# Chunked SSD outputs: log of dt in the exponent, the mask on GpSimd, u times v stored as one product, and earlier chunk loads

## The chip, the cores and the metric

The kernel runs on one core of one Trainium2 chip. The core has five instruction queues that run beside each other, each in its own fixed order: TensorE (PE, with its weight loads as PEld), VectorE (DVE), ScalarE (ACT), GpSimd (POOL) and SyncE (SP), which here only issues transfers. The metric is the device time of one execution in microseconds (us). The order on each queue is settled when the program is built, by a list scheduler that works with priorities, so a change in one place can reorder others.

## The reference

One layer of a two-stream trunk over 256 context tokens and 1024 latent tokens, D = 1024, float32: modulated RMSNorm, one input projection whose columns feed three mixers (Mamba-2 SSD, chunked spatial gating, S5), an output projection, a squared-ReLU MLP, a final norm. The change concerns two of the mixers. The SSD mixer, per direction and chunk of 128 tokens:

```
dt   = softplus(s[..., OFF_DT:OFF_SGU] + ssd_dt_bias)
a_cum = cumsum(dt * a)                                  # within a chunk
lmat = exp(where(lower, a_cum[q] - a_cum[k], -inf))
y_diag = sum_k (cm[q] . bm[k]) * lmat[q, k] * (x[k] * dt[k])
y_off  = (cm[q] . h_prev) * exp(a_cum[q])
h      = exp(a_cum[-1]) * h_prev + sum_k bm[k] * exp(a_cum[-1] - a_cum[k]) * x[k] * dt[k]
```

Both directions are summed (the backward one is masked the other way), and D times x is added. The gating mixer returns `u * mix`, with `mix = W_s v + b` per chunk and head.

## The kernel before, in words

Tokens lie along the free axis in ten chunks of 128; features lie on the partitions. A *slab* is 128 output columns of a projection for all 1280 tokens: 24 matmuls of 256 columns and 48 of 512 (`proj_tile`, three products of split operands for each of eight k).

Around the change the program runs: the v and dt projection (`vdt`), the spatial mix (`sgu_mix`), two slabs for u (`u_slab`), the S5 scans (`s5_main`, eight rounds), four xBC slabs (`xbc_slab`) and `dt_chain`, which makes dt and its running sums. Then `ssd_group` for two groups of four heads. Each group has a pass `right` that builds the backward states and a pass `outputs` over ten chunks. Group 0 is drawn first, four more xBC slabs stand between its two passes, and z slabs, the S5 gate, two mixed tiles (`mixed_tile`) and the first output-projection slabs are emitted among the output chunks. The code's order sets priorities; the scheduler interleaves.

One output chunk does this. It loads `xc` (x, B, C of the chunk) and `rb`, the running sums of both directions as rows, copied to all partitions: 512 KB from the DRAM tile `rows_d`. ACT makes `er = exp(rb)`. The decay matrix is the exponent min(row 0 - col 0, row 1 - col 1): per head one ACT shift of row 1 and one DVE subtract-and-min, then one ACT exponential over 128x512. The matmul B.C lands in PSUM (`pcb`); DVE multiplies it with the two triangular masks (`cm`), and per head ACT scales the one with dt of the forward direction and DVE adds the other scaled with dt of the backward one. DVE multiplies decay and this, and `rb[:, 1]` feeds four matmuls into `py` (tile ps_wb). `po` is the states' part; DVE multiplies it with `er`, POOL adds its two directions, DVE adds all into `cm`, which is stored to `y_d`. The forward state `hf` goes on to the next chunk: POOL scales it, DVE adds the new part.

Buffers: `rb` has 3, `xc` 5, `cm` 2. `rb` is held until the matmuls into `py` have read it. All these loads and the store go through SP's one queue in order. The mix goes to the DRAM tile `mix_d` in ten stores, gelu(u) to `u_d` from ACT's queue, and `mixed_tile` loads both and multiplies them.

In the profile every `tensor_tensor` has line 54, every `scalar_tensor_tensor` line 57, every activation line 60 and every DMA line 48, since helpers record them; they are told apart by their tiles.

Of the kernel before, what the change touches and what calls it, by code (L numbers as in the profile page):

```python
# [18 lines left out]
KD = 8  # L19
# [23 lines left out]
def trunk_kernel(ctx: ExitStack, tc: tile.TileContext, I, O):  # L43
# [3 lines left out]
    def load(dst, src, eng=None):  # L47
        (eng or nc.sync).dma_start(out=dst, in_=src)
# [190 lines left out]
    def ev(name, dt=F32):  # L239
        return evp.tile([128, 512], dt, tag="ev", name=name, bufs=7)  # L240
# [467 lines left out]

    def sgu_mix():
        for v in va:  # L710
            act(v, v, ACT.Gelu_apprx_tanh)
        for c in range(NCH):
            vq = ev("vq")[:, 0:256]
            act(vq, va[c // 5][:, c % 5, :], ACT.Square, accum_out=vss[:, c:c + 1])
        rstd(vss, vr, 256)
        for c in range(NCH):
            v = va[c // 5][:, c % 5, :]
            V.tensor_scalar(out=v, in0=v, scalar1=vr[:, c:c + 1], scalar2=None, op0=ALU.mult)
            pm = bank("mm", 2)
# [3 lines left out]
            mx = ev("vq")[:, 0:256].rearrange("p (a b) -> p a b", a=2)  # L723
            for a in range(2):
                stt(mx[:, a, :], pm[:, a * 128:(a + 1) * 128], sgug[:, a:a + 1], sgub[:, a, :], ALU.mult, ALU.add)
            load(mix_d.rearrange("(a p) n -> p a n", p=128)[:, :, c * 128:(c + 1) * 128], mx)

# [6 lines left out]
    def dt_chain():  # L734
# [32 lines left out]
        T.matmul(pc[:, 320:480], lhsT=ones, rhs=dta.rearrange("p d c -> p (d c)"), start=True, stop=True)  # L767
        S.copy(col[:, 0], pc[:, 0:80])
        act(col[:, 1], pc[:, 80:160], ACT.Copy, scale=-1.0)
        act(wdec.rearrange("p d c -> p (d c)"), pc[:, 160:320], ACT.Exp)  # L770
# [10 lines left out]

    def u_slab(m):
# [45 lines left out]

    def ssd_group(pool, g):

        hb = {1: None}

        def chunk_xbc(c, n):
            o = xoff(c)
            xc = pool.tile([128, 4, 128], F32, tag="xc", name="xc", bufs=5)[:, 0:n]
            load(xc, xbc_d[g, 0:n, :, o:o + 128].rearrange("a p n -> p a n"))
            return xc

        def scal(t, d, c):
            return t[:, d, c * 8 + g * 4:c * 8 + g * 4 + 4]  # L840
# [28 lines left out]
        def right():  # L869
            px, bt, _ = tok_major(chunk_xbc(1, 3))  # L870
            hb[0] = new_state(f"hb{g}", 9, 1, 1, px, bt, None, "hb")
# [4 lines left out]
            hb[9] = init(1, f"hb{g}", 9)  # L876
            yield
            for c in range(9, 2, -1):
                px, bt, _ = tok_major(chunk_xbc(c, 3))
                hb[c - 1] = new_state(f"hb{g}", 9, 1, c, px, bt, hb[c], "hb")  # L880
                yield

        def outputs():
            hf = None
            for c in range(NCH):
# [19 lines left out]
                cm = pool.tile([128, 2, 128], F32, tag="cm", name="cm", bufs=2)  # L905
                tt(cm, pcb.unsqueeze(1).to_broadcast([128, 2, 128]), tri[:, 0:2], ALU.mult)

                d0, d1 = scal(DTD, 0, c), scal(DTD, 1, c)
                for hh in range(4):
                    act(rb[:, 0, hh], cm[:, 0], ACT.Copy, scale=d0[:, hh:hh + 1])  # L910
                    stt(rb[:, 0, hh], cm[:, 1], d1[:, hh:hh + 1], rb[:, 0, hh], ALU.mult, ALU.add)
                tt(rb[:, 1], rb[:, 1], rb[:, 0], ALU.mult)
                xs = pool.tile([128, 4, 64], F32, tag="xs", name="xs", bufs=2)
                S.copy(xs, px)
                py = bank("wb", 2)[:, 0:256].rearrange("p (a q) -> p a q", a=2)
                for a in range(2):
                    for par in range(2):
                        T.matmul(py[par * 64:(par + 1) * 64, a, :], lhsT=xs[:, 2 * a + par], rhs=rb[:, 1, 2 * a + par],
                                 start=True, stop=True)
# [22 lines left out]
    def mixed_tile(t):  # L942
# [62 lines left out]
    with tc.tile_pool(name="pv", bufs=1) as pv, tc.tile_pool(name="p5", bufs=1) as p5, ExitStack() as stk:  # L1005
# [44 lines left out]
        V.tensor_scalar(out=glubh, in0=glub, scalar1=0.5, scalar2=None, op0=ALU.mult)  # L1050
        sgu_mix()
        for m in range(2):
            u_slab(m)
        for _ in prep:
# [21 lines left out]
    with tc.tile_pool(name="pd", bufs=1) as pd, banks("psB"):  # L1076
        (right0, out0), (right1, out1) = [ssd_group(pd, g) for g in range(2)]
        def drain(g):
# [536 lines left out]
```

## Time and profile before

| | us |
|---|---|
| median of 3 runs (lowest to highest) | 1580.24 (1580.15 to 1582.12) |
| the profiled execution | 1578.67 |
| its span on the core | 1576.7 |

| stretch (us from the span's start) | what runs | PE busy | granted clock, of full |
|---|---|---|---|
| 190 to 320 | S5 scans, xBC slabs | 121.82 of 130 | 0.97 |
| 320 to 390 | backward states of group 0, xBC and z slabs | 67.16 of 70 | 1.00 |
| 390 to 593 | the twenty output chunks, with z slabs and mixed tiles | 156.25 of 203 | 0.83 |
| 593 to 690 | output projection, second norm | 94.47 of 97 | 1.00 |

From 800 us on the MLP runs, with PE busy nearly throughout. The granted clock is a mean over the stretch; its levels are 1.2 and 2.4 GHz.

### The profile page before, as it was taken

Reading aid. Unit: us, or ns where it says so; the run is one execution under the profiler, and the core shown is the slowest. Engines: PE = TensorE matmul, PEld = TensorE weight load, DVE = VectorE, ACT = ScalarE, POOL = GpSimd, SP = SyncE. Lnnn points to the kernel's source line nnn. Section 1 sums busy time; section 2 is a strip of 40 time slices with the busy share of each in tenths; the row PEclk is TensorE's granted clock in tenths of the full one; section 3 lists DMA queues with packets and bytes.
Section 4 is the critical chain, followed back from the end, with each engine's and each line's share of the span. In section 5 each row is a group of like instructions: output and inputs, shape, how many; then the busy total and the mean of one; then the engine's idle time right before and its main releaser. Section 6 shows DMA issues by size and latency. Waiting matters only on the chain.

```text
span 1576.7 us, 23817 instructions
## 1 busy us (share of the span) xinstructions
PE 1423.4 (90%) x8360; PEld 1202.6 (76%) x8360; DVE 1067.9 (68%) x1929; ACT 751.1 (48%) x1541; POOL 389.5 (25%) x487
## 2 busy tenths in 40 slices
PE   4689898999787779989999999999899999999795
PEld 3567676778565568878888888888788888887795
DVE  5773368668667885558977764674564768979945
ACT  3643434456645753437655554554555334424322
POOL 4555466613011122321100000000241313032033
PEclk9699999999997879999999999999999999999897
DMA  9759785264675647346444443344744245315312
GB/s 326 251 174 252 227 285 159 88 171 119 181 228 149 172 145 236 122 123 195 138 158 149 149 139 116 125 148 151 250 149 146 70 158 174 121 54 182 112 35 100
DMA packets 238903, 253.29 MB, mean 161 GB/s; under 512 B 15648, under 2 KB 163136, under 8 KB 238784
## 3 DMA queue, kind: packets, MB, share of 16 engines
q1 hardware_dynamic: 222880, 234.51, 48.2%
q10 hardware_dynamic: 15904, 17.27, 3.4%
q8 instruction: 66, 1.08, 0.3%
q14 instruction: 53, 0.43, 0.1%
HBM read 182.82 MB, written 68.89 MB: 160 GB/s over the span
## 4 chain that ended last, share of the span: by engine, by line
PE 58%; DVE 8%; DMA 6%; ACT 2%; issue 2%; POOL 1%; SPq 0%; DVEq 0%; ACTq 0%; POOLq 0%
PE ps_w L1215 7%; PE ps_w L1213 7%; PE ps_w L1214 7%; PE ps_w L1369 6%; PE ps_w L1370 6%; PE ps_w L1371 6%; PE ps_mm L219 4%; PE ps_mm L221 4%; PE ps_mm L220 4%; DMA rb<-rows_d 2%; PE ps_mm L1371 1%; PE ps_mm L1370 1%; PE ps_mm L1369 1%; DVE X L54 1%; DVE rb L57 1%
## 5 line engine op out<-in xcount | busy, mean ns | idle before, releaser
L219 PE MATMUL ps_mm<-hi,wh 128*128 128x512 f32 (+1 forms) x576 | 211.6, 367 | 20.1 <-DVE dtr L707 16.0
L221 PE MATMUL ps_mm<-hi,wl 128*128 128x512 f32 (+1 forms) x576 | 209.4, 364 | 0.9 <-DVE wl L54 0.9
L220 PE MATMUL ps_mm<-lo,wh 128*128 128x512 f32 (+1 forms) x576 | 209.8, 364 | 0.0
L1369 PE MATMUL ps_w<-uB,uA 128*128 128x512 f32 (+1 forms) x520 | 190.6, 371 | 9.3 <-ACT uB L60 8.9
L1370 PE MATMUL ps_w<-uB,uA 128*128 128x512 f32 (+1 forms) x520 | 191.3, 368 | 7.9 <-DVE uB L54 7.9
L1371 PE MATMUL ps_w<-uB,uA 128*128 128x512 f32 (+1 forms) x520 | 190.2, 367 | 0.0
L54 POOL TENSOR_TENSOR cb<-h 128x512 f32<-128x512 f32 x14 | 21.9, 1571 | 512.7 <-DMA h<-w 402.4
L219 PEld LDWEIGHTS ps_mm<-hi,wh 128*128 128x128 f32 x576 | 111.2, 193 | 38.1 <-DVE dtr L707 16.8
L221 PEld LDWEIGHTS ps_mm<-hi,wl 128*128 128x128 f32 x576 | 111.0, 193 | 18.1 <-DVE wl L54 1.8
L220 PEld LDWEIGHTS ps_mm<-lo,wh 128*128 128x128 f32 x576 | 111.0, 193 | 15.0 <-issue 0.6
L1369 PEld LDWEIGHTS ps_w<-uB,uA 128*128 128x128 f32 x520 | 99.9, 193 | 25.2 <-ACT uB L60 9.3
L1370 PEld LDWEIGHTS ps_w<-uB,uA 128*128 128x128 f32 x520 | 100.2, 193 | 24.7 <-DVE uB L54 9.8
L1371 PEld LDWEIGHTS ps_w<-uB,uA 128*128 128x128 f32 x520 | 99.8, 192 | 15.5
L60 ACT ACTIVATE uB<-tb 128x512 fp32r<-128x512 f32 x106 | 65.9, 625 | 64.9 <-PE ps_w L1371 31.7
L54 DVE TENSOR_TENSOR uB<-tb,uB 128x512 fp32r<-128x512 f32 x106 | 87.6, 846 | 13.1 <-ACT uB L60 13.1
L54 DVE TENSOR_TENSOR X<-X,ps_w 128x512 f32<-128x512 f32 x84 | 56.1, 680 | 27.7 <-PE ps_w L1371 27.6
L54 DVE TENSOR_TENSOR q<-q,ps_w 128x512 f32<-128x512 f32 x48 | 32.9, 685 | 59.7 <-PE ps_w L1215 59.0
L54 DVE TENSOR_TENSOR wl<-wraw,wh 128x1024 fp32r<-128x1024 f32 x32 | 48.4, 1514 | 36.7 <-ACT wh L60 35.9
L60 ACT ACTIVATE c<-c 128x512 f32<-128x512 f32 x64 | 40.3, 629 | 57.8 <-DVE c L54 56.9
L1371 PE MATMUL ps_mm<-ch,uA 128*128 128x256 f32 x224 | 63.2, 283 | 0.0
L1370 PE MATMUL ps_mm<-cl,uA 128*128 128x256 f32 x224 | 63.2, 283 | 0.0
L1369 PE MATMUL ps_mm<-ch,uA 128*128 128x256 f32 x224 | 63.1, 283 | 0.0
(435 smaller groups left out, 3875.3 us busy)
## 6 DMA issues: line engine op xcount, KB each, us to landing
rw<-w SPq DMA_DIRECT2D x112, 256.0 KB
tb<-a_d SPq DMA_DIRECT2D x106, 256.0 KB
aw<-ada_w SPq DMA_DIRECT2D x64, 256.0 KB
h<-w SPq DMA_DIRECT2D x32, 512.0 KB
a_d<-t SPq DMA_DIRECT2D x42, 256.0 KB
rb<-rows_d SPq DMA_DIRECT2D x20, 512.0 KB
adaw<-ada_w SPq DMA_DIRECT2D x32, 256.0 KB
wraw<-w_out SPq DMA_DIRECT2D x16, 512.0 KB
```

Of the source, the lines that this page charges most:

```text
L54: eng.tensor_tensor(out=out, in0=a, in1=b, op=op)
L57: V.scalar_tensor_tensor(out=out, in0=a, scalar=sc, in1=b, op0=op0, op1=op1)
L60: S.activation(out=out, in_=in_, func=func, **kw)
L219: T.matmul(out, lhsT=wh(k), rhs=xh(k), start=(k == 0), stop=False)
L220: T.matmul(out, lhsT=wh(k), rhs=xl(k), start=False, stop=False)
L221: T.matmul(out, lhsT=wl(k), rhs=xh(k), start=False, stop=(k == nk - 1))
L1213: T.matmul(out, lhsT=wh, rhs=X[0][:, j, :], start=(j == 0), stop=False)
L1214: T.matmul(out, lhsT=wh, rhs=X[1][:, j, :], start=False, stop=False)
L1215: T.matmul(out, lhsT=wl, rhs=X[0][:, j, :], start=False, stop=(j == 3))
L1369: T.matmul(out, lhsT=wh, rhs=bh, start=start, stop=False)
L1370: T.matmul(out, lhsT=wh, rhs=bl, start=False, stop=False)
L1371: T.matmul(out, lhsT=wl, rhs=bh, start=False, stop=stop)
```

## The change

The exponent now carries log dt: `col` holds log(max(dt, 1e-37)) minus the running sum, for both directions. The mask is an additive tile `cap`, 0 where a pair counts and -1e30 where it doesn't, added to the rows by POOL, a direction at a time. ACT takes the exponential per head and direction with `col` as its bias; DVE adds the two directions and multiplies by B.C from PSUM. The result lies in `sg` (2 buffers), not in `rb`; `rb` has 2 buffers instead of 3, and is read only by POOL and by the exponentials for `er`. `cm` has 3 buffers instead of 2, and both groups' backward states share one ring of 16. The chunk loads of `xc` and `rb` get a priority 600 higher. The mix stays in SBUF, in two buffers of the pool that held x; `u_slab` multiplies it in and stores the product once, through SP's queue; `mixed_tile` loads one tile where it loaded two and multiplied.

```diff
-    def sgu_mix():
+    def sgu_mix(px):
+        mix = [px.tile([128, KD, 256], F32, tag="x", name="mix", bufs=2).rearrange("p k n -> p (k n)")[:, 0:NT]
+               for _ in range(2)]
...
-            load(mix_d.rearrange("(a p) n -> p a n", p=128)[:, :, c * 128:(c + 1) * 128], mx)
...
+        V.tensor_scalar(out=col, in0=DTD, scalar1=1e-37, scalar2=None, op0=ALU.max)
+        act(col, col, ACT.Ln)
+        fl = col.rearrange("p d c -> p (d c)")
+        tt(fl, fl, pc[:, 0:160], ALU.subtract)
...
             act(us, p, ACT.Gelu_apprx_tanh)
-            load(u_d[m * 128:(m + 1) * 128, t0:t0 + n], us, nc.scalar)
+            tt(us, us, mix[m][:, t0:t0 + n], ALU.mult)
+            load(um_d[m * 128:(m + 1) * 128, t0:t0 + n], us)
...
-                rb = pool.tile([128, 2, 4, 128], F32, tag="rb", name="rb", bufs=3)
-                load(rb, rows_d[:, c * 8 + g * 4:c * 8 + g * 4 + 4, :].partition_broadcast(128))
-                cf, cbk = scal(col, 0, c), scal(col, 1, c)
+                rb = pool.tile([128, 2, 4, 128], F32, tag="rb", name="rb", bufs=2)
+                with tc.high_priority(offset=600):
+                    load(rb, rows_d[:, c * 8 + g * 4:c * 8 + g * 4 + 4, :].partition_broadcast(128))
+                sg = pool.tile([128, 2, 4, 128], F32, tag="sg", name="sg", bufs=2)
+                for d in range(2):
+                    tt(sg[:, d], rb[:, d], cap[:, d].unsqueeze(1).to_broadcast([128, 4, 128]), ALU.add, G)
...
-                for hh in range(4):
-                    act(rb[:, 1, hh], rb[:, 1, hh], ACT.Identity, bias=cbk[:, hh:hh + 1])
-                    stt(rb[:, 1, hh], rb[:, 0, hh], cf[:, hh:hh + 1], rb[:, 1, hh], ALU.subtract, ALU.min)
-                act(rb[:, 1], rb[:, 1], ACT.Exp)
+                for d in range(2):
+                    cd = scal(col, d, c)
+                    for hh in range(4):
+                        act(sg[:, d, hh], sg[:, d, hh], ACT.Exp, bias=cd[:, hh:hh + 1])
+                tt(sg[:, 0], sg[:, 0], sg[:, 1], ALU.add)
...
-                tt(cm, pcb.unsqueeze(1).to_broadcast([128, 2, 128]), tri[:, 0:2], ALU.mult)
-                for hh in range(4):
-                    act(rb[:, 0, hh], cm[:, 0], ACT.Copy, scale=d0[:, hh:hh + 1])
-                    stt(rb[:, 0, hh], cm[:, 1], d1[:, hh:hh + 1], rb[:, 0, hh], ALU.mult, ALU.add)
-                tt(rb[:, 1], rb[:, 1], rb[:, 0], ALU.mult)
+                tt(sg[:, 0], pcb.unsqueeze(1).to_broadcast([128, 4, 128]), sg[:, 0], ALU.mult)
...
-            load(mx, mix_d[k * 128:(k + 1) * 128, t0:t0 + n])
-            tt(u, u, mx, ALU.mult)
...
+        cap = pd.tile([128, 2, 128], F32, name="cap")
+        V.tensor_scalar(out=cap, in0=tri[:, 0:2], scalar1=-1.0, scalar2=1e30, op0=ALU.add, op1=ALU.mult)
```

The order on every queue is the same up to the spatial mix and again from the second norm on. Between them it differs. On POOL, in the output pass of group 1 (er: the states' part; hf: the forward state; sq: the mixed tile's norm), before:

```order
L54 TENSOR_TENSOR hf<-hf,dtot 128x256
L54 TENSOR_TENSOR sq<-sq,z 128x256
L54 TENSOR_TENSOR er<-er 128x256
L54 TENSOR_TENSOR sq<-sq,z 128x256
L54 TENSOR_TENSOR hf<-hf,dtot 128x256
L54 TENSOR_TENSOR er<-er 128x256
L54 TENSOR_TENSOR hf<-hf,dtot 128x256
```

And now, around the same mixed tile:

```order
L54 TENSOR_TENSOR sg<-rb,cap 128x512 x2
L54 TENSOR_TENSOR sq<-sq,z 128x256
L54 TENSOR_TENSOR er<-er 128x256
L54 TENSOR_TENSOR hf<-hf,dtot 128x256
L54 TENSOR_TENSOR sq<-sq,z 128x256
L54 TENSOR_TENSOR sg<-rb,cap 128x512 x2
L54 TENSOR_TENSOR er<-er 128x256
L54 TENSOR_TENSOR hf<-hf,dtot 128x256
L54 TENSOR_TENSOR sg<-rb,cap 128x512 x2
```

Two adds of 128x512 stand in front of each chunk's `er` and `hf`; eight of the forty stand ahead of the first `hf`.

On PE, at the last output chunk (ps_wb: its matmuls; ps_mm with hi and wh: slab matmuls, three to each k), before:

```order
L219 MATMUL ps_mm<-hi_5688,wh 128x512
L220 MATMUL ps_mm<-lo_5689,wh 128x512
L221 MATMUL ps_mm<-hi_5688,wl 128x512
L918 MATMUL ps_wb<-rb,xs 64x128 x4
L925 MATMUL ps_wb<-xc,hf 128x128 x2
L925 MATMUL ps_wb<-xc,h_4442 128x128 x2
L219 MATMUL ps_mm<-hi_5688,wh 128x512
```

And now:

```order
L922 MATMUL ps_wb<-sg,xs 64x128 x4
L929 MATMUL ps_wb<-xc,hf 128x128 x2
L929 MATMUL ps_wb<-xc,hb 128x128 x2
L860 MATMUL ps_ws<-xw,bt 128x256
L922 MATMUL ps_wb<-sg,xs 64x128 x4
L929 MATMUL ps_wb<-xc,hf 128x128 x2
L929 MATMUL ps_wb<-xc,h_4396 128x128 x2
L199 MATMUL ps_mm<-ones,sq 128x1 x4
L204 MATMUL ps_mm<-pk_87,rt 128x128 x4
L218 MATMUL ps_mm<-hi_5231,wh 128x256
```

No slab matmul stands between the last chunks any more. Counted over PE's whole order, 72 slab matmuls of 256 columns and 32 of 512 leave the stretch between the first and the last chunk's matmuls; 24 and 5 of them now stand ahead of it, 48 and 27 behind it. The first matmul of the S5 scans stands 24 and 83 slab matmuls later than before, since the S5 pool takes the memory that the mix holds.

On SP, around the first stored output chunks, before:

```order
L48 DMA rb<-rows_d 128x2x512
L48 DMA xc<-xbc_d 128x4x128
L48 DMA y_d<-cm 128x2x128
L48 DMA ssdo<-hf 128x256
L48 DMA xbc_d<-xbc 128x1284
L48 DMA yf<-y_d 128x1288
L48 DMA rb<-rows_d 128x2x512
```

And now:

```order
L48 DMA xc<-xbc_d 128x4x128
L48 DMA y_d<-cm 128x2x128
L48 DMA rb<-rows_d 128x2x512 x2
L48 DMA z_d<-ze 128x512
L48 DMA xc<-xbc_d 128x3x128
```

Four row loads stand ahead of the first store in both; behind it came one, and now come two, so each further row load stands a chunk earlier against the stores.

## Rows read from the trace of the kernel before

**Rows 1.** The page, section 1: busy time, share, instructions of each engine.

```profile
PE 1423.4 (90%) x8360; PEld 1202.6 (76%) x8360; DVE 1067.9 (68%) x1929; ACT 751.1 (48%) x1541; POOL 389.5 (25%) x487
```

**Rows 2.** Busy times by stretch; behind them granted clock, DMA share, GB/s.

```profile
core 0: us, PE busy (x) PEld busy (x) DVE busy (x) ACT busy (x) POOL busy (x), PEclk, DMA share, GB/s
190.00:320.00 130.00, 121.82 (x844) 98.38 (x843) 91.96 (x156) 50.27 (x123) 77.73 (x105) 0.97 0.57 178
390.00:593.00 203.00, 156.25 (x824) 122.28 (x821) 149.34 (x378) 122.88 (x299) 38.75 (x48) 0.83 0.64 174
...
800.00:900.00 100.00, 100.00 (x431) 80.56 (x430) 73.12 (x119) 54.19 (x93) 0.00 (x0) 1.00 0.44 148
```

**Rows 3.** The chain that ended last, 390 to 593: by line; start, us, what.

```profile
by line: DMA rb<-rows_d 13.5%; DVE rb L57 7.9%; issue 5.5%; PE ps_mm L219 4.6%; PE ps_mm L220 4.5%; PE ps_mm L661 4.5%; PE ps_mm L221 4.3%; DMA y_d<-cm 3.5%; PE ps_ws L854 3.4%; PE ps_wb L925 3.4%; PE ps_wb L918 3.2%; DMA z<-z_d 3.2%; POOL 
...
441.92 9.97 DMA rb<-rows_d
458.13 5.97 DMA rb<-rows_d
```

**Rows 4.** Groups on DVE, 390 to 593: busy us, mean ns, idle before.

```profile
L57 DVE SCALAR_TENSOR_TENSOR rb<-cm,DTD,rb 128x128 f32<-128x128 f32 x73 | 24.0, 371 | 4.2 <-ACT rb L60 4.2
L57 DVE SCALAR_TENSOR_TENSOR rb<-rb,col 128x128 f32<-128x128 f32 x68 | 23.5, 386 | 12.0 <-ACT rb L60 12.0
L54 DVE TENSOR_TENSOR rb<-rb 128x512 f32<-128x512 f32 x19 | 14.8, 777 | 0.0
...
L54 DVE TENSOR_TENSOR er<-ps_wb,er 128x512 f32<-128x512 f32 x16 | 11.0, 685 | 4.9 <-PE ps_wb L925 4.9
...
L54 DVE TENSOR_TENSOR cm<-ps_wa,pk 128x256 f32<-128x256 f32 x18 | 7.6, 420 | 9.3 <-DMA y_d<-cm 8.9 <-PE ps_wa L904 0.4
```

**Rows 5.** Groups on ACT, 390 to 593.

```profile
L60 ACT ACTIVATE rb<-cm,DTD 128x128 f32<-128x128 f32 x72 | 22.9, 389 | 2.2 <-DVE cm L54 2.2
L60 ACT ACTIVATE rb<-rb,col 128x128 f32<-128x128 f32 x68 | 22.3, 391 | 0.4
L60 ACT ACTIVATE er<-rb 64x512 f32<-64x512 f32 x34 | 21.3, 627 | 24.6 <-DMA rb<-rows_d 23.6 <-DVE cm L54 0.4
L60 ACT ACTIVATE rb<-rb 128x512 f32<-128x512 f32 x17 | 10.7, 630 | 4.1 <-DVE rb L57 4.0
```

**Rows 6.** Groups on POOL: the whole span, then 390 to 593.

```profile
L54 POOL TENSOR_TENSOR sq<-sq 128x512 f32<-128x512 f32 x16 | 23.9, 1498 | 41.4 <-ACT sq L60 40.9
L54 POOL TENSOR_TENSOR er<-er 128x256 f32<-128x256 f32 x16 | 12.4, 774 | 50.9 <-DVE er L54 41.5 <-ACT rb L60 9.4
L54 POOL TENSOR_TENSOR hf<-hf,dtot 128x256 f32<-128x256 f32 x14 | 9.0, 644 | 64.2 <-DVE y L57 13.3 <-PE ps_wb L925 11.3 <-DVE rb L57 11.0
```

**Rows 7.** Instructions of DVE, then of POOL, in order of time: start, us.

```profile
517.48 0.41 DVE L57 SCALAR_TENSOR_TENSOR y<-z,y 128x256 f32<-128x256 f32 x1
517.82 1.21 DVE L54 TENSOR_TENSOR rb<-rb 128x512 f32<-128x512 f32 x1
518.95 0.41 DVE L54 TENSOR_TENSOR hf<-hf,ps_ws 128x256 f32<-128x256 f32 x1
...
517.58 0.90 POOL L54 TENSOR_TENSOR er<-er 128x256 f32<-128x256 f32 x1
518.49 1.12 POOL L54 TENSOR_TENSOR sq<-sq,z 128x256 f32<-128x256 f32 x1
```

**Rows 8.** Tile t, whole span: duration of one in ns, min/median/max.

```profile
L54 POOL TENSOR_TENSOR t<-acc x4: 1362/1580/7653, 717.5 to 753.6; 128x512 f32<-128x512 f32 x4
```

**Rows 9.** Who waited for whom, 390 to 593: us in total, times, longest.

```profile
ACT er L60 <- DMA rb<-rows_d: 23.6, 9, 5.3
PE ps_ws L854 <- DVE xw L54: 23.4, 8, 4.7
```

More of the change, by code (lines that the diff above doesn't have):

```diff
@@ L722, in sgu_mix @@
                          lhsT=v[:, h * 64:(h + 1) * 64], rhs=sguw[:, h, :], start=True, stop=True)
-            mx = ev("vq")[:, 0:256].rearrange("p (a b) -> p a b", a=2)
             for a in range(2):
-                stt(mx[:, a, :], pm[:, a * 128:(a + 1) * 128], sgug[:, a:a + 1], sgub[:, a, :], ALU.mult, ALU.add)
-            load(mix_d.rearrange("(a p) n -> p a n", p=128)[:, :, c * 128:(c + 1) * 128], mx)
+                stt(mix[a][:, c * 128:(c + 1) * 128], pm[:, a * 128:(a + 1) * 128], sgug[:, a:a + 1], sgub[:, a, :],
+                    ALU.mult, ALU.add)
+        return mix
     DTD = cst.tile([128, 2, 80], F32, name="DTD")
@@ L778, in dt_chain, with u_slab @@
         load(rows_d.rearrange("d c q -> c d q"), rws[0:80, :, :])
-    def u_slab(m):
+    def u_slab(m, mix):
         w = wslab(I["w_in"][:, 1552 + m * 128:1552 + (m + 1) * 128])
@@ L825, in xbc_slab, with ssd_group @@
         load(xbc_d[g, a], acc)
-    def ssd_group(pool, g):
+    def ssd_group(pool, g, cap):
         hb = {1: None}
@@ L870, in right @@
             px, bt, _ = tok_major(chunk_xbc(1, 3))
-            hb[0] = new_state(f"hb{g}", 9, 1, 1, px, bt, None, "hb")
+            hb[0] = new_state("hb", 16, 1, 1, px, bt, None, "hb")
             yield
@@ L875, in right @@
             load(O["ssdo"][:, 512 + g * 256:512 + (g + 1) * 256], hbf)
-            hb[9] = init(1, f"hb{g}", 9)
+            hb[9] = init(1, "hb", 16)
             yield
@@ L889, in outputs @@
                 xc = chunk_xbc(c, 4)
-                rb = pool.tile([128, 2, 4, 128], F32, tag="rb", name="rb", bufs=3)
-                load(rb, rows_d[:, c * 8 + g * 4:c * 8 + g * 4 + 4, :].partition_broadcast(128))
-                cf, cbk = scal(col, 0, c), scal(col, 1, c)
+                rb = pool.tile([128, 2, 4, 128], F32, tag="rb", name="rb", bufs=2)
+                with tc.high_priority(offset=600):
+                    load(rb, rows_d[:, c * 8 + g * 4:c * 8 + g * 4 + 4, :].partition_broadcast(128))
+                sg = pool.tile([128, 2, 4, 128], F32, tag="sg", name="sg", bufs=2)
+                for d in range(2):
+                    tt(sg[:, d], rb[:, d], cap[:, d].unsqueeze(1).to_broadcast([128, 4, 128]), ALU.add, G)
                 er = pool.tile([128, 2, 2, 128], F32, tag="er", name="er", bufs=3)
@@ L917, in outputs @@
                     for par in range(2):
-                        T.matmul(py[par * 64:(par + 1) * 64, a, :], lhsT=xs[:, 2 * a + par], rhs=rb[:, 1, 2 * a + par],
+                        T.matmul(py[par * 64:(par + 1) * 64, a, :], lhsT=xs[:, 2 * a + par], rhs=sg[:, 0, 2 * a + par],
                                  start=True, stop=True)
@@ L927, in outputs @@
                 tt(er[:, ds], po[:, ds], er[:, ds], ALU.mult)
+                cm = pool.tile([128, 2, 128], F32, tag="cm", name="cm", bufs=3)
                 for a in range(2):
@@ L956, in mixed_tile @@
         for k in range(2):
-            u, mx = ev("u")[:, :n], ev("mx")[:, :n]
-            load(u, u_d[k * 128:(k + 1) * 128, t0:t0 + n])
-            load(mx, mix_d[k * 128:(k + 1) * 128, t0:t0 + n])
-            tt(u, u, mx, ALU.mult)
+            u = ev("u")[:, :n]
+            load(u, um_d[k * 128:(k + 1) * 128, t0:t0 + n])
             split(hi[t][:, 4 + k, :], lo[t][:, 4 + k, :], u)
@@ L1050, in trunk_kernel @@
         V.tensor_scalar(out=glubh, in0=glub, scalar1=0.5, scalar2=None, op0=ALU.mult)
-        sgu_mix()
+        mix = sgu_mix(px)
         for m in range(2):
-            u_slab(m)
+            u_slab(m, mix)
         for _ in prep:
@@ L1076, in trunk_kernel @@
     with tc.tile_pool(name="pd", bufs=1) as pd, banks("psB"):
-        (right0, out0), (right1, out1) = [ssd_group(pd, g) for g in range(2)]
+        cap = pd.tile([128, 2, 128], F32, name="cap")
+        V.tensor_scalar(out=cap, in0=tri[:, 0:2], scalar1=-1.0, scalar2=1e30, op0=ALU.add, op1=ALU.mult)
+        (right0, out0), (right1, out1) = [ssd_group(pd, g, cap) for g in range(2)]
         def drain(g):
```

11 lines of the change are left out of this document (3 added, 8 removed).

## Prediction

> **What bounds the kernel now.** I read the page's busy shares first, then the busy times by stretch, the chain of waits in the stretch that stands out, and there the groups by engine. PE is busy for 1423.4 us of 1576.7 [rows 1], so 153 us at most can come from filling PE, and the rest only from its clock. The MLP offers nothing: from 800 to 900 us PE is busy for all of it at full clock [rows 2]. The stretch that stands out is 390 to 593 us, the twenty output chunks: PE is busy for 156.25 of 203 us and the granted clock is 0.83, a mix of its two levels [rows 2]. The busiest engine beside it is DVE with 149.34 us, 74% of the stretch, then ACT with 122.88; POOL has 38.75. In the chain that ended last, the wait for the row loads has 13.5% of the stretch (27.4 us), DVE's per-head instructions on rb 7.9% (16.0 us), and the store of cm, which holds one of two buffers, 3.5% (7.1 us); single loads show up with 6 and 10 us [rows 3]. ACT stood still for rows in nine places, 23.6 us, and PE for DVE's xw in eight, 23.4 us, which says that DVE comes late [rows 9]. So in this stretch the pace is DVE's work per chunk and the late row loads, and PE idles. The matmuls are the same before and after, so what the change can win is PE's idle time and low clock here.
>
> **The change part by part.** The sum is made against the profiled execution, 1578.67 us, of which the span is 1576.7; the median of the runs is 1580.24, which is 1.6 us more.
>
> DVE in the stretch: out go the two per-head groups, 24.0 and 23.5 us, and the masking of B.C, 7.6 us [rows 4], together 55.1. The add of the two directions takes the place of rb times rb (same shape, both inputs in SBUF, 14.8 us). The multiplication by B.C is new, from PSUM as er is: 20 by 685 ns is 13.7 us [rows 4]. The multiplication of u by the mix leaves the mixed tiles and appears in the u slabs, at the same sizes, so I cost it at nothing; in the u slabs it lies beside 72 matmuls each, and if that cover fails it costs six instructions of at most 0.78 us, rb times rb's mean [rows 4]. Net, DVE falls by 41 us to about 108.
>
> ACT: eight small copies and shifts per chunk leave, 389 and 391 ns each, and eight small exponentials come. A small exponential has no row; the big one takes 630 ns for 512 columns and er 627 ns, what a shift of that width could also be expected to cost, so I take 390 ns and cost this at nothing [rows 5]. The bounds are 0.16 us (a quarter of 630) and 0.63 us each, that is 37 us less or 38 us more over 160. What surely leaves is the exponential over 512 columns: 17 in this stretch, 10.7 us [rows 5]. ACT falls to 112 us and becomes the busiest engine beside PE.
>
> POOL: forty adds of 128x512 with a repeated operand. The nearest row is an add of that shape, 1498 ns [rows 6]; I take 1.5 us, between 0.77 us (the 128x256 add of er, if the repeated operand came free) and 3 us (twice). Eight of the forty stand ahead of the first hf in the order, so 32 fall in the stretch: 48 us, and POOL rises to 87. Per chunk that is 3.0 us of adds beside 0.77 of er and 0.64 of hf [rows 6], 4.4 us, and its queue is in order: behind an add that waits for rows stand er and hf of the chunk before, and behind hf the next chunk's matmuls into po. A loaded chunk needs 4.4 us of POOL, 5.6 us of ACT (112 over twenty, slabs and mixed tiles included), so neither sets a pace slower than the present ten us per chunk (203 over twenty).
>
> Is there a price for POOL and DVE together? At 517.82 us DVE's rb times rb took 1.21 us; its group's mean is 777 ns. It began 0.24 us into POOL's er (517.58 to 518.48) and ended 0.55 us after that; POOL's next instruction ended 0.58 us after DVE's [rows 7]. Each seems to have stood still while the other ran. The Trainium skill, SBUF — State Buffer, section Who interferes with whom, says just this: a DVE instruction with two SBUF inputs and a GpSimd instruction that reads SBUF exclude each other for a whole instruction, and whoever comes second waits. The rule speaks against moving the mask to GpSimd, and the rows agree with it. But it cuts both ways here. Of the DVE instructions with two SBUF inputs, eight per chunk leave, and of the big ones one stays (sg plus sg); the new product reads PSUM. If each of the forty adds held DVE off by half its length once, that would be 30 us of DVE on 108, still under the present 149. I take 2 us for it on the path.
>
> Loads: a row buffer was held until the chunk's last use by PE; it is now free after POOL's adds and two exponentials, 3.0 plus 1.25 us after landing, and with two sg buffers the next chunks' work can be one step further ahead. In SP's order the row loads stand a chunk earlier against the stores. The loads with 6 and 10 us [rows 3] then start a chunk (some seven us) earlier, and most of the 27.4 us can go. The third cm buffer takes the 7.1 us of the store. The log for col adds one small activation and two DVE instructions of 160 columns outside the stretch, under 2 us, beside slab matmuls.
>
> The new length of the stretch, in two ways. By engines: DVE ran at 74% of the stretch; if ACT, then the busiest, is used as well as that, 112 / 0.736 = 152 us. By the chain: 203 less 27.4, 16.0 and 7.1 is 152.5. I take 155, with the 2 us of POOL and DVE.
>
> What is given back: the order moves slab matmuls out of the stretch. A slab matmul of 512 columns costs 100 us / 431 = 0.232 us at full clock [rows 2], one of 256 half. Ahead of the stretch 24 and 5 are added, 3.9 us, and behind it 48 and 27, 11.8 us; PE is nearly full in both places, so 15.8 us come back as they are. The S5 scans begin 24 and 83 slab matmuls later, 22 us of PE's time, because their memory holds the mix; the u and xBC slabs cover it, and I take 2 us for what POOL (77.73 us busy of 130 [rows 2]) then does more densely; if that cover fails, I take as much again as PE idles there now, 8 us.
>
> Sum: 203 - 155 - 15.8 - 2 = 30 us less: 1578.7 - 30 = 1548.7, and 1.6 us to the median: 1550 us.
>
> **The rivals.** First, the stretch packs better: with full row buffers PE does not idle, the clock stays at the upper level, and the 156 busy us at 0.83 shrink. The stretch cannot fall under ACT's 112 us; at 90% of it, 125 us, the time is 1550 - 30 = 1520. For it: the stretch would become dense on every engine but POOL. Against: the last five chunks have no slab matmul between them, so there PE waits for the chain whatever the others do.
>
> Second, most is given back: the chunks are paced by the forward state's loop (po, er on DVE, POOL's er add, POOL's hf, DVE's add), which is unchanged but for two 1.5 us adds in POOL's queue inside it. If that costs 1 us per chunk, 20 us of the 50 are lost, and the time is 1570; at 32 us lost it is 1582, no change. For it: PE's 23.4 us of waiting is on xw and the states [rows 9]. Against: POOL has 115 us free in the stretch.
>
> Third, it is slower: POOL's adds are held off by DVE. One 128x512 add on POOL took 7.65 us where the median is 1.58 [rows 8]. With d us per add POOL has 38.75 + 32 d us in the stretch, and used at 0.736 of the time it sets the stretch alone. The stretch may be 187 us before the 15.8 us given back eat all; that is where POOL has 138 us and d is 3.1 us. At 3.5 us the stretch is 205 us and the time 1580 + 2 + 16 + 2 = 1600. For it: adds beside a DVE at 70% are common. Against: DVE's instructions left in the chunk mostly read PSUM.
>
> Last, the loads may not come earlier at all: two buffers instead of three, in an in-order queue. Then the 27.4 us stay, the stretch is 182 us, and the time 1577, hardly a change; I count it with the second.
>
> **How the numbers follow.** The forecast, 1530 to 1568 us: 0.55. Better packing, 1505 to 1530: 0.15. Mostly given back, 1568 to 1584: 0.18. Slower by POOL, 1584 to 1610: 0.12. A run of this kernel tells 0.2% (3 us) from no change; 0.06 of the second case lies within 1577 to 1583.4, and 0.12 is slower, so faster has 0.82. The range leaves out the outer part of the first rival and nearly all of the third: 1516 to 1584.
>
> **What would show it.** Between the first and last chunk's ps_wb matmuls about 155 us instead of 200. There: DVE near 108 us busy, ACT near 112, POOL near 87, sg adds of 1.5 us mean; waits for rows under 8 us; granted clock 0.85 or more. Behind it 12 us more of dense slab work; the MLP unchanged. I am wrong if sg adds mean over 3 us, if er still waits 20 us for rows, if an exponential of 128 columns takes 0.6 us, or if PE stands idle for more than 10 us more between 190 and 390.

## The result and the profile after

| | before | after |
|---|---|---|
| median (lowest to highest), us | 1581.18 (1580.15 to 1582.43), 4 runs | 1563.11 (1561.95 to 1566.61), 4 runs |
| span of the profiled execution, us | 1576.7 | 1560.1 |
| first ps_wb matmul at, us | 389.7 | 405.3 |
| from there to the last ps_wb matmul, us | 200.9 | 157.3 |
| from there to the end, us | 986.1 | 997.5 |

The ratio is 0.9889, with a 95% interval of 0.9871 to 0.9907. The changed kernel is 18 us faster; 30 were forecast. The span cut at the first and the last ps_wb matmul shows what came in: the output chunks take 43.6 us less, the part ahead of them 15.6 us more, the part behind them 11.4 us more, together 16.6 us less.

The changed kernel's page, section 1, answers to [rows 1]:

```profile
PE 1412.6 (91%) x8360; PEld 1194.2 (77%) x8360; DVE 1049.6 (67%) x1772; ACT 738.4 (47%) x1518; POOL 456.1 (29%) x527
```

Busy times of the changed kernel by stretch (columns as in [rows 2]): ahead of the chunks, the chunks, 20 us behind them, a piece of the MLP, and last a piece of the S5 rounds:

```profile
190.00:405.30 215.30, 197.37 (x1236) 161.73 (x1234) 147.88 (x212) 96.20 (x195) 117.03 (x130) 0.97 0.55 166
405.30:562.60 157.30, 122.07 (x700) 95.53 (x699) 110.29 (x211) 100.67 (x269) 83.72 (x81) 0.89 0.68 195
562.60:582.60 20.00, 19.38 (x119) 17.22 (x118) 12.14 (x21) 7.79 (x14) 1.46 (x2) 1.00 0.87 282
800.00:900.00 100.00, 100.00 (x430) 80.60 (x429) 73.13 (x119) 53.60 (x93) 0.00 (x0) 1.00 0.44 148
...
220.00:345.00 125.00, 111.43 (x729) 90.03 (x728) 104.77 (x159) 55.67 (x124) 89.48 (x109) 0.97 0.50 157
```

The same view of the kernel before, cut at its own first and last ps_wb, with 20 us behind them:

```profile
190.00:389.70 199.70, 188.68 (x1200) 154.93 (x1198) 141.84 (x218) 91.16 (x196) 96.33 (x125) 0.98 0.56 169
389.70:590.60 200.90, 154.15 (x815) 120.59 (x815) 148.09 (x375) 123.18 (x300) 36.53 (x47) 0.83 0.64 174
590.60:610.60 20.00, 20.00 (x114) 17.50 (x113) 8.08 (x13) 4.62 (x8) 6.61 (x6) 1.00 0.86 289
```

In the chunks DVE does 110 us in place of 148, ACT 101 in place of 123, POOL 84 in place of 37; PE's share rises little (78% from 77%), but the granted clock rises from 0.83 to 0.89. Ahead of them PE stands idle for 17.9 us in place of 11.0, and the MLP is what it was.

Groups of instructions in the changed kernel, 380 to 600 us (as [rows 4 to 6]):

```profile
L54 POOL TENSOR_TENSOR sg<-rb,cap 128x512 f32<-128x512 f32 x36 | 50.0, 1410 | 29.9 <-PE ps_wb L922 25.4 <-issue 4.6
L60 ACT ACTIVATE sg<-sg,col 128x128 f32<-128x128 f32 x144 | 45.8, 390 | 14.5 <-POOL sg L54 14.4
L60 ACT ACTIVATE er<-rb 64x512 f32<-64x512 f32 x34 | 21.4, 628 | 12.3 <-DVE cm L54 9.5 <-DMA rb<-rows_d 2.5
L54 DVE TENSOR_TENSOR sg<-sg 128x512 f32<-128x512 f32 x18 | 17.6, 975 | 10.3 <-ACT sg L60 9.9 <-POOL sg L54 0.2
L54 DVE TENSOR_TENSOR sg<-ps_wa,sg 128x512 f32<-128x512 f32 x20 | 13.7, 683 | 4.2 <-PE ps_wa L915 3.9
```

The small exponential takes 390 ns and the product with B.C 683 ns, as taken. ACT's wait for rows, 23.6 us in [rows 9], is 2.5.

The chain in the changed kernel's chunks, by line (as in [rows 3]):

```profile
by line: issue 12.2%; POOL sg L54 8.8%; ACT sg L60 8.6%; PE ps_wb L922 6.4%; PE ps_wb L929 6.1%; ACT er L60 5.4%; DMA z<-z_d 5.3%; DMA u<-um_d 4.1%; DMA yf<-y_d 3.9%; DMA rb<-rows_d 3.8%; PE ps_ws L860 2.8%; DVE mo L57 2.6%; DVE cm L54 2.3%
```

Rows fell from 13.5% to 3.8%, the store of cm and the per-head DVE work are gone, and nothing has more than an eighth: the chunk is now a chain through all engines.

The late part is the one ahead. The S5 matmuls on XT and on Ht, kernel before and then changed kernel (ns min/median/max, first and last start in us):

```profile
L592 PE MATMUL ps_w<-u,XT x128: 299/302/536, 192.0 to 290.8; 128*64 128x163 f32 x128
...
L637 PE MATMUL ps_w<-Ht,Y x64: 297/300/404, 206.0 to 317.3; 128*128 128x161 f32 x64
```

```profile
L591 PE MATMUL ps_w<-u,XT x128: 299/302/353, 218.1 to 311.6; 128*64 128x163 f32 x128
...
L636 PE MATMUL ps_w<-Ht,Y x64: 297/299/404, 230.1 to 342.4; 128*128 128x161 f32 x64
```

The S5 rounds take 125.3 us in the one and 124.3 in the other, though the first starts 26 us earlier. They run at a length of their own, and a late start is a late end.

### The profile page after: what moved, and what is told of

Its sections match the earlier page's. It is cut to its first block, busy times and chain, and to the rows that moved or that the text cites. A ratio compares the mean times of both kernels' runs of the same rounds, so it can differ in the third digit from the quotient of the medians.

```text
span 1560.1 us, 23640 instructions
## 1 busy us (share of the span) xinstructions
PE 1412.6 (91%) x8360; PEld 1194.2 (77%) x8360; DVE 1049.6 (67%) x1772; ACT 738.4 (47%) x1518; POOL 456.1 (29%) x527
## 4 chain that ended last, share of the span: by engine, by line
PE 55%; DVE 11%; DMA 5%; issue 4%; ACT 4%; POOL 4%; SPq 0%; DVEq 0%; ACTq 0%; POOLq 0%
PE ps_w L1220 7%; PE ps_w L1218 7%; PE ps_w L1219 7%; PE ps_w L1374 6%; PE ps_w L1375 6%; PE ps_w L1376 6%; PE ps_mm L220 3%; PE ps_mm L218 3%; PE ps_mm L219 3%; DVE X L54 2%; PE ps_mm L1375 1%; PE ps_mm L1376 1%; PE ps_mm L1374 1%; POOL sg L54 1%; DVE xbc L57 1%
## 5 line engine op out<-in xcount | busy, mean ns | idle before, releaser
L1375 PEld LDWEIGHTS ps_w<-uB,uA 128*128 128x128 f32 x520 | 99.7, 192 | 24.6 <-DVE uB L54 9.9
L54 POOL TENSOR_TENSOR sg<-rb,cap 128x512 f32<-128x512 f32 x40 | 56.3, 1428 | 38.5 <-PE ps_wb L922 25.4
L1376 PE MATMUL ps_mm<-ch,uA 128*128 128x256 f32 x224 | 63.2, 283 | 0.0
```

The costliest lines, as they stand in the source:

```text
L54: eng.tensor_tensor(out=out, in0=a, in1=b, op=op)
L1375: T.matmul(out, lhsT=wh, rhs=bl, start=False, stop=False)
L1376: T.matmul(out, lhsT=wl, rhs=bh, start=False, stop=stop)
```

## The experiments

Theory A: what is missing is lost ahead of the chunks, because the mix lies in memory that the S5 tables need. Rivals: the new dt chain, the raised loads, or GpSimd's additions take it. In the expectations the changed kernel's stretch is counted to its last py matmul, 155.7 us, and the part behind it accordingly, 999; the figures below go to the last ps_wb matmul of all, as in the table above. Ratios are to the kernel before.

**The u times mix part undone.** `um_undone`: the changed kernel, with

```
-            tt(us, us, mix[m][:, t0:t0 + n], ALU.mult)
-            load(um_d[m * 128:(m + 1) * 128, t0:t0 + n], us)
+            load(u_d[m * 128:(m + 1) * 128, t0:t0 + n], us, nc.scalar)
```

and the mix stored to `mix_d`, loaded and multiplied in the mixed tiles, as before.

> The changed kernel with the u times mix part undone: gelu(u) and the mix are stored apart again and multiplied in the mixed tiles; the chunk's new arithmetic, the mask on GpSimd and the load priorities stay. Theory A (the missing 10 us are the S5 scans' late start, because the mix lies in the memory that the S5 tables need): the first S5 matmul on XT falls back from 218 to about 192 us, the first chunk's ps_wb from 405 to 385 to 393 us (the order has 8 us less slab work ahead of it than the changed kernel, and the 26 us of the scans' delay are gone), the stretch from first to last chunk grows from 155.7 to 156 to 164 us, since 8 us of slab work come back into it, and the time is 1547 to 1556 us. Rival B (the late first chunk comes from the new dt chain or from the raised loads): the first ps_wb stays within 4 us of 405 and the time within 3 us of 1563.

1557.29 us, ratio 0.9863 (0.9847 to 0.988). XT and the chunks behave as A says, stretch 158.4 us. First XT to last ps_wb of this run:

```profile
L592 PE MATMUL ps_w<-u,XT x128: 299/302/532, 193.0 to 292.2; 128*64 128x163 f32 x128
...
L920 PE MATMUL ps_wb<-sg,xs x160: 272/273/477, 387.3 to 543.2; 128*64 128x128 f32 x160
...
L927 PE MATMUL ps_wb<-xc,h x16: 275/346/422, 400.8 to 545.7; 128*128 128x128 f32 x16
```

So the part costs 18.0 us ahead of the chunks. In PE's order this version also has 8.1 us of slab matmuls fewer ahead of them and 8.1 more among them than the changed kernel (at the prediction's price for a slab matmul), and among them these cost its stretch 1.1 us, so some of the 18.0 us is slab work that changed its place. But the time falls by only 6 us, a little short of A: behind the chunks this version takes 1010.6 us against 997.5. Its first 20 us there, to be read against the third row of the changed kernel above, and the pieces of its chain in them (start, us, what):

```profile
545.70:565.70 20.00, 11.60 (x68) 10.80 (x67) 11.05 (x17) 7.21 (x13) 2.73 (x3) 0.74 0.73 243
```

```profile
551.02 2.74 DMA mx<-mix_d
...
553.84 0.70 DVE u L54
...
555.95 5.27 DMA m<-m_d
```

PE is busy for 11.6 us where it was 19.4: the second mixed tile is not ready when the last chunk ends, and the load of the mix is on its chain, with the load of the S5 result behind it. The part of the change is thus a trade: 18 us paid ahead, some of 13 us won behind.

**The part alone.** `um_alone`: the kernel before with this part only (the reverse of the diff above).

> The kernel before with only the u times mix part of the change: the mix stays on the chip, the product is stored once. Theory A: first XT matmul near 218 us instead of 192, first ps_wb at 400 to 406 us instead of 390, the chunk stretch at 195 to 201 us (it loses 10 us of slab matmuls, but DVE and the row loads set its pace), the part behind it as before: 1586 to 1596 us in all, slower than before. Rival B (this part is harmless or a gain by itself, with six multiplications and six loads fewer in the mixed tiles): 1576 to 1583 us.

1601.13 us, ratio 1.0148 (1.0124 to 1.0173): 23 us slower, 5 more than A's range reaches; the rival is out. XT starts at 216.4 us, the first ps_wb matmul at 414.5 us, 24.8 us later than before; the stretch has 198.7 us, the part behind 985.6 us, as before. The late S5 start arrives whole, and nothing is won behind: in the kernel before, with its longer chunks, PE was busy for all of the first 20 us behind them, and there was nothing to win there.

**Only the place of the mix.** `mix_through_dram`: the changed kernel, with the mix stored to DRAM and loaded again for the product at u's projection:

```
+            mx = ev("mx")[:, :n]
+            load(mx, mix_d[m * 128:(m + 1) * 128, t0:t0 + n])
+            tt(us, us, mx, ALU.mult)
```

> The changed kernel, in which only the place of the mix differs: it is stored to DRAM in ten pieces as before and loaded again for the product at u's projection, so that the S5 tables' memory is free early. Theory A (it is the memory): first XT matmul near 192 us, first ps_wb at 385 to 394 us, stretch 156 to 165 us, time 1547 to 1557 us, about that of the version with the whole part undone. Rival B (it is the product at the projection, its DVE instructions or its stores in SP's queue): first ps_wb near 405 and time within 4 us of 1563.

1566.88 us, ratio 0.9923 (0.9907 to 0.994). The places came as A says, XT at 192.5 and ps_wb at 392.6 us, the time as B says. From 190 to 220 us in this run:

```profile
190.00:220.00 30.00, 24.73 (x171) 19.09 (x171) 14.82 (x30) 5.98 (x13) 6.57 (x9) 0.87 0.75 241
```

PE idles 5.3 us here, where the changed kernel has all 30 us busy, and the stretch is 169.6 us. In PE's order 12.8 us more slab matmuls stand inside the stretch than in the changed kernel, and 12.8 us fewer ahead of it. That memory alone brings S5 forward is shown, since the product and its stores in SP's queue stay as in the changed kernel; the way through DRAM costs as much again, and whether by its loads or by the new places of the slab matmuls is open.

**The mix in v's place.** `mix_in_v`: each chunk's mix overwrites its v, which only that chunk's matmuls read; no other memory, no way through DRAM:

```
-                stt(mix[a][:, c * 128:(c + 1) * 128], pm[:, a * 128:(a + 1) * 128], ...
+                stt(v[:, a * 128:(a + 1) * 128], pm[:, a * 128:(a + 1) * 128], ...
...
+                tt(uv, uv, va[c // 5][:, c % 5:c % 5 + b - c, m * 128:(m + 1) * 128], ALU.mult)
```

> The changed kernel, in which the mix of a chunk overwrites the chunk's v, which its matmuls have read, instead of lying in the memory that the S5 tables need; u times mix is formed at u's projection and stored once, as in the changed kernel, in eight multiplications instead of six, and nothing goes through DRAM in between. Theory A2 (the product has two sides: the late S5 start ahead of the chunks, and 11.5 us less behind them, since the mixed tile that ends last then loads one tile fewer): first XT matmul near 192 us, first ps_wb at 385 to 392 us as where the part is undone, stretch 154 to 162 us, the part behind it 997 to 1002 us as in the changed kernel, time 1540 to 1553 us, faster than the changed kernel and than the one without the part. Rival F (the part behind grows whenever the chunks come earlier, because other loads or slabs then stand late): the part behind is 1008 to 1012 us and the time 1554 to 1560 us.

1549.08 us, ratio 0.9804 (0.9782 to 0.9826), below both kernels and the fastest of all. Its stretches, ahead, the chunks, and 20 us behind:

```profile
190.00:389.40 199.40, 190.22 (x1213) 157.37 (x1211) 142.32 (x208) 90.23 (x188) 101.92 (x129) 0.98 0.57 175
389.40:545.10 155.70, 124.15 (x732) 96.53 (x732) 108.84 (x210) 103.64 (x271) 84.78 (x81) 0.92 0.69 200
545.10:565.10 20.00, 17.41 (x94) 15.99 (x93) 10.72 (x19) 8.61 (x14) 3.12 (x3) 0.75 0.74 241
```

The chunks begin at 389.4 us, PE idles 9.2 us ahead of them, and 15.9 of the 18.0 us are there. The part behind has 1005.1 us, between A2's 997 to 1002 and F's 1008 to 1012: of the 13.1 us that the product wins there, 5.5 are kept. Why not more was not tested.

**GpSimd or DVE for the mask.** `mask_on_dve` is the changed kernel, `mix_in_v_dve` the one just shown, with

```
-                    tt(sg[:, d], rb[:, d], cap[:, d].unsqueeze(1).to_broadcast([128, 4, 128]), ALU.add, G)
+                    tt(sg[:, d], rb[:, d], cap[:, d].unsqueeze(1).to_broadcast([128, 4, 128]), ALU.add)
```

> The changed kernel with the forty mask additions on VectorE instead of GpSimd. Theory A (DVE's work set the old pace, and 32 additions of 0.8 us or so in the stretch, 25 us, bring DVE from 109 back to 134 us busy): the stretch grows from 156 to 175 to 185 us and the time to 1580 to 1592 us. Rival C (GpSimd's additions in front of er's addition and of hf in its queue cost as much as they save, and DVE has room at 70%): stretch 150 to 160 us, time 1557 to 1566 us.

> The version with the mix in v's place, with the forty mask additions on VectorE instead of GpSimd. Theory K (GpSimd for the mask is worth some 6 us, as the 1569 against 1563 us of the changed kernel with this edit say): stretch 157 to 164 us, time 1552 to 1559 us. Rival C (DVE has the room, and the difference was chance of the order): time within 4 us of 1549 us or below.

1569.26 us, ratio 0.9933 (0.9914 to 0.9953), and 1556.62 us, ratio 0.9861 (0.9845 to 0.9877). By the medians GpSimd is worth 6 us on the one base and 8 on the other: less than theory A of the first run (17 or more), more than its rival C, and the time that K gives. The traces do not show where. The profiled execution of `mask_on_dve` was its fastest, 1561.66 us, as short as the changed kernel's 1561.95, and its stretch, with the same slab matmuls in it by PE's order, is 159.9 us, in C's range. That of `mix_in_v_dve` is 174.5 us, 10 above K's range; its chunks begin 6.0 us earlier than in `mix_in_v`, and the part behind them is 5.5 us shorter. The stretch of `mask_on_dve`, its groups from 380 to 600 us, and last a group of the changed kernel:

```profile
401.20:561.10 159.90, 125.34 (x708) 98.23 (x707) 119.31 (x245) 102.42 (x270) 36.88 (x45) 0.87 0.69 195
```

```profile
L54 DVE TENSOR_TENSOR sg<-rb,cap 128x512 f32<-128x512 f32 x36 | 24.6, 721 | 0.0
...
L54 DVE TENSOR_TENSOR sg<-ps_wa,sg 128x512 f32<-128x512 f32 x20 | 13.6, 682 | 3.9 <-PE ps_wa L915 3.8
L54 DVE TENSOR_TENSOR sg<-sg 128x512 f32<-128x512 f32 x18 | 13.2, 735 | 10.9 <-ACT sg L60 10.8
...
L54 DVE TENSOR_TENSOR cm<-cm,er 128x256 f32<-128x256 f32 x20 | 10.2, 512 | 0.4 <-POOL er L54 0.4
```

```profile
L54 DVE TENSOR_TENSOR cm<-cm,er 128x256 f32<-128x256 f32 x20 | 13.3, 663 | 2.2 <-POOL er L54 2.1
```

The addition takes half as long on DVE, 721 against 1410 ns, and adds 24.6 us to DVE. Yet DVE's busy time in the stretch grows by only 9.0 us, from 110.29 to 119.31, mostly because its other instructions get shorter. With the additions on GpSimd DVE's sg plus sg takes 975 ns in place of 735, 18 by 0.24 = 4.3 us, and cm plus er, which also has both inputs in SBUF, 663 in place of 512, 20 by 0.15 = 3.0 us. That is the price of the two engines side by side in each chunk, 7.3 us for these two groups.

**What the raised priority does.** `priority_alone` is the kernel before with the priority of the chunk loads alone; `arith_alone` is `um_undone` without it:

```
+            with tc.high_priority(offset=600):
+                load(xc, xbc_d[g, 0:n, :, o:o + 128].rearrange("a p n -> p a n"))
...
+                with tc.high_priority(offset=600):
+                    load(rb, rows_d[:, c * 8 + g * 4:c * 8 + g * 4 + 4, :].partition_broadcast(128))
```

> The kernel before with nothing changed but the raised priority of the chunk loads xc and rb. Theory D (the late row loads set much of the old pace, and a place earlier in SP's queue mends it): the stretch falls from 200.8 us to 170 to 185 us, the part behind grows by the 5.4 us of slab matmuls that the order moves there, and the time is 1562 to 1575 us. Rival E (a row buffer is held until the chunk's last matmuls have read it, so that a load cannot start earlier, whatever its place; the new arithmetic's early release is what counts): stretch 190 to 201 us, time 1574 to 1586 us.

> The kernel before with the chunk's new arithmetic and mask on GpSimd alone: without the raised load priority and without the product of u and the mix. Theory D: the loads stand late again, the stretch is 168 to 185 us instead of 158, and the time is 1566 to 1580 us. Rival E (the early release of the row buffer and the shorter DVE work are enough): stretch within 5 us of 158, the time within 4 us of the 1557 us of the version that has the priority too.

1578.75 us, ratio 0.999 (0.9976 to 1.0004), and 1557.21 us, ratio 0.9854 (0.983 to 0.9879), as with the priority; stretches 195.9 and 161.4 us. It does nothing measurable to the time in either. The rows still come late in `priority_alone`:

```profile
ACT er L60 <- DMA rb<-rows_d: 23.7, 7, 6.3
```

Before it was 23.6 us. A load that waits for its buffer is not helped by its place in the queue. Theory D is out.

**What the early release does.** `early_release` is the kernel before, its old arithmetic writing into a tile of its own (rb 2 buffers, sg 2; both groups' backward states share a ring of 16, as in the changed kernel); `in_place` is `um_undone` done in the row buffer (rb 3, no sg):

```
-                    stt(rb[:, 1, hh], rb[:, 0, hh], cf[:, hh:hh + 1], rb[:, 1, hh], ALU.subtract, ALU.min)
+                    stt(sg[:, 1, hh], rb[:, 0, hh], cf[:, hh:hh + 1], sg[:, 1, hh], ALU.subtract, ALU.min)
```

> The kernel before with its old arithmetic and no raised priority, but with the decay matrix built in a tile sg of its own (two buffers; rb has two instead of three), so that the row buffer is free after er and the per-head shifts instead of after the chunk's last matmuls. Theory I (the held row buffer made the row loads late, and that set the old pace): the stretch from first to last chunk falls from 200.8 us to 165 to 182 us, waits for rows in it from 27 us of the chain to under 8, and the time, with 6 us of slab matmuls moved behind, to 1560 to 1574 us. Rival J (the sixteen small instructions per chunk that DVE and ACT hand to each other set it): stretch 188 to 200 us, time 1574 to 1586 us.

> The counterpart: the new arithmetic, with the raised priority and without the product of u and the mix, but done in the row buffer itself (three rb buffers, no sg), so that a row buffer is held to the end of the chunk as before and the mask waits for er. Theory I: the rows come late again, the stretch is 180 to 198 us instead of 158 and the time 1576 to 1594 us. Rival J (the smaller arithmetic is what counts): stretch 156 to 168 us and time 1554 to 1566 us.

1582.1 us, ratio 1.0028 (1.0015 to 1.0042), and 1565.83 us, ratio 0.9914 (0.9896 to 0.9932); stretches 194.7 and 167.9 us. Both sit with rival J: the arithmetic counts for more than the release, which by itself makes the kernel 0.3% slower. With the new arithmetic, working in a tile of its own is worth more: `um_undone` is 9.5 us shorter in the stretch and 8.5 in time than `in_place`. The chain in the stretch of `early_release` says what came in the rows' place:

```profile
by line: DMA y_d<-cm 18.7%; DVE sg L57 13.8%; issue 11.1%; DMA z<-z_d 7.1%; PE ps_ws L854 4.5%; PE ps_wb L919 4.0%; DVE cm L54 3.6%; ACT sg L60 3.4%; PE ps_wb L926 3.0%; DVE er L54 2.9%; DVE cm L57 2.8%; DVE y L57 2.7%; PE ps_wa L845 2.7%; 
```

Its waits for rows, and those of `in_place`, with the mask's wait for er there:

```profile
ACT er L60 <- DMA rb<-rows_d: 5.0, 3, 2.5
```

```profile
POOL rb L54 <- ACT er L60: 42.9, 15, 5.1
...
ACT er L60 <- DMA rb<-rows_d: 14.6, 7, 7.6
```

The rows are mended by the early release, from 23.6 to 5.0 us. Then the store of cm, out of two buffers, has 36 us of the chain. In `in_place` the mask waits 42.9 us for er, which must read the rows before they are overwritten, so the 9.5 us are not the late rows' alone.

**The store of cm as well.** `early_release_cm3` adds the third cm buffer to it.

```
-                cm = pool.tile([128, 2, 128], F32, tag="cm", name="cm", bufs=2)
+                cm = pool.tile([128, 2, 128], F32, tag="cm", name="cm", bufs=3)
```

> The kernel before with the old arithmetic in a tile sg of its own, as in the run early_release, and a third buffer for cm. There the waits for rows were 5.0 us, but the store of cm had 18.7% of the stretch's chain, 36 us, and the stretch was 194.7 us. Theory L (the store of cm out of two buffers took the place of the row loads; with both gone the stretch shrinks with the old arithmetic too): stretch 165 to 182 us, time 1560 to 1572 us. Rival J (the small instructions that DVE and ACT hand to each other come next and hold it): the store leaves the chain, but the stretch is 186 to 197 us and the time 1574 to 1585 us.

1571.24 us, ratio 0.994 (0.9919 to 0.9962), the time as L says, the stretch 183.0 us, 1 us outside L's range. What is late next in it (wait, and the busy times of the stretch):

```profile
PE ps_ws L854 <- DVE xw L54: 33.8, 8, 7.6
```

```profile
392.10:575.10 183.00, 136.45 (x788) 108.10 (x788) 146.18 (x371) 120.71 (x298) 37.71 (x45) 0.86 0.63 183
```

DVE is now busy for 80% of the stretch, and PE waits for its xw. Less work on DVE is what is left to do, and the new arithmetic does it.

**One more sg buffer.** `mix_in_v_sg`: `mix_in_v` with three buffers for the forward half of sg, because POOL waited 25.4 us for one in the changed kernel.

```
-                sg = pool.tile([128, 2, 4, 128], F32, tag="sg", name="sg", bufs=2)
+                sg = [pool.tile([128, 4, 128], F32, tag=f"sg{d}", name=f"sg{d}", bufs=3 - d) for d in range(2)]
```

> The same kernel with the mix in v's place and three buffers instead of two for the forward direction's sg, so that one more chunk's mask and exponentials can be ahead (hb has 14 buffers instead of 16 for the room). Theory G (the two sg buffers hold the stretch back: POOL's additions waited 25 us for the ps_wb matmuls that read them in the changed kernel): the stretch falls from 156 to 140 to 150 us and the time to 6 to 14 us below the version with two. Rival H (those waits lie off the path, since ACT, DVE and PE are handed on in a chain in each chunk): stretch within 4 us and time within 4 us of the version with two.

1566.73 us, ratio 0.9917 (0.9892 to 0.9942): 18 us slower than with two, which neither theory had. Two waits of it in the stretch:

```profile
POOL sg L54 <- DMA rb<-rows_d: 33.8, 11, 5.7
...
POOL sg L54 <- PE ps_wb L924: 12.0, 6, 7.8
```

POOL waits less for sg (16.7 us in `mix_in_v`) and more for rows, for which `mix_in_v` shows no wait in the stretch: with sg free, the two row buffers seem short. The stretch has 164.1 us, the part behind 1012.1. How much of it is hb's 14 buffers, which changed too, or the 3.0 us more of slab matmuls that PE's order has in the stretch, is open.

## Why the prediction was right or wrong

**The chunks: right in sum, wrong in its parts.** First to last ps_wb was forecast at 155 instead of 200 us; it is 157.3 instead of 200.9. The sum took 203 to 155, 48 us, where 43.6 came: its window held 2 us more than the stretch. That the sum fits is in part luck. Both of its ways gave 152 us, and neither holds: the first had ACT as the busiest engine, used for 74% of the stretch, but DVE stayed the busiest, with 70%, and ACT has 64%. Of engines, DVE was forecast at 108 (110.3), ACT at 112 (100.7), POOL at 87 (83.7), an addition on POOL at 1.5 us (1.41), the small exponential at 0.39 (0.390), the clock at 0.85 or more (0.89), rows under 8 us (2.5). The second way's shares of the chain gave 27.4 us to the rows, 7.1 to the store and 16.0 to the per-head work. The runs give, one after the other, 6.2 us to the early release (200.9 to 194.7), 11.7 to the third cm buffer (to 183.0), and 21.6 to 24.6 to the new arithmetic with the mask on GpSimd (to 161.4 or 158.4). A share of the chain is no gain: with the rows gone, the store stood where they had stood, and with the store gone, DVE. Nor is the whole of each step a gain: in PE's order the stretch holds 54.8 us of slab matmuls before, 48.5 in both early-release versions and 47.1 in the two last, so the first 6.2 us are no more than the slabs moved out. And the split holds in this order only: with the new arithmetic first, the tile of its own is worth 9.5 us (`in_place` to `um_undone`, with 47.1 us of slabs in both).

**The loads: wrong in the means.** "In SP's order the row loads stand a chunk earlier" was to bring them forward. `priority_alone` and `arith_alone` show that this does nothing; the early release, named in the same paragraph, does it.

**POOL beside DVE: right in kind, dearer than taken.** I took 2 us on the path, with 30 us on DVE as the bound if each addition held it once. DVE pays 4.3 us in sg plus sg and 3.0 in cm plus er, which the prediction left out; what reaches the path no run shows by itself. The exclusion is there (sg plus sg 735 to 975 ns), as the Trainium skill, SBUF — State Buffer, section Who interferes with whom, states it; but the new product of each chunk reads PSUM, and takes 683 ns with the additions beside it and 682 without. The rival in which POOL's additions make it slower would have needed 3.1 us each.

**The slab matmuls moved: right in number, in part by luck.** 11.8 us were forecast behind the chunks, 11.4 came. But the multiplication costed "at nothing" hides a term here: without the product, and with the same slab matmuls behind the chunks, that part is 13.1 us longer (`um_undone`, 24.5 more than before), since the shorter stretch lays the second mixed tile bare. Two terms that the sum lacked, the bare tile and the product that mends it, nearly cancel.

**The S5 start: wrong, the step that failed.** The prediction knew that the scans begin "22 us of PE's time" later, "because their memory holds the mix"; XT begins 26 us later. It went on: "the u and xBC slabs cover it, and I take 2 us", 8 if the cover fails. With the 3.9 us of slabs that is 5.9 us ahead of the chunks; 15.6 came. The mistake is what the cover covers. Slabs fill PE while S5 runs, but the S5 rounds need some 124 us from whenever they start, though PE is busy for 111.43 of 125 us beside them in the changed kernel, and the chunks' matmuls stand behind them. What stood between the end of S5 and the first chunk, 72.4 us, shrank by 9.5, and S5 took 1.0 less; the other 15.6 us were passed on. In them PE is idle for 6.9 us more and busy for 8.7 more, of which the forecast's slabs are 3.9; where the other 4.8 lie is open. The prediction's own sign, over 10 us more of idle PE between 190 and 390 us, did not show: it was 6.9. `um_alone`, in which nothing shrank, pays 24.8. The 8 us for a failed cover were taken from PE's idle time before, which says what PE could lose there, not what a late chain costs. This step is 9.7 us of the 13.7 by which the sum was off, the chunks the other 4.4, the part behind 0.4 the other way.

The rivals: packing did not go beyond the forecast, the mask did not cost what the second rival had it cost (it gains), and the time, 1563, lies in the forecast's own range, at its far side. Most of what is missing from the 30 us was lost ahead of the chunks, which no rival named.

## What to carry to other kernels

When a value is kept on the chip instead of being stored, ask whose memory it sits in, and who starts only when that is free; a chain with a length of its own passes a late start on, and work that fills the engine beside it does not shorten it. A buffer that nobody needs any more (here v, once read) takes the value, and S5 began 3 us later than before instead of 26. Read the chain's shares as a list of what is late next, not as terms of a sum, and free a buffer earlier before you raise the priority of the load that waits for it.

## What was not expected of the hardware

One addition over 128x512 on GpSimd with a repeated second operand took 1259 ns at least and 1284 in the median, no more than a plain one: in the kernel before, sq plus sq of that shape took 1.29 and 1.26 us at 693.66 and 699.10 us, and 2.07 at 678.96, so the 1498 ns of [rows 6] are a mean with longer instructions in it. In the changed kernel the mean was 1410; an estimate of what GpSimd itself paid for working beside DVE is then 36 by 0.126 = 4.5 us, beside DVE's 7.3. The additions of the changed kernel (ns min/median/max, first and last start in us):

```profile
L54 POOL TENSOR_TENSOR sg<-rb,cap x40: 1259/1284/2547, 355.1 to 549.8; 128x512 f32<-128x512 f32 x40
```
